# A decoder layer on one core: TensorE's instructions pinned to program order in the attention stage, and the column-tiled products gathered

## The chip, the cores and the metric

The kernel runs on 1 core of one Trainium2 chip. The metric is the device time of one execution in microseconds (us); the figure of the kernel before is the median of 3 runs.

## The reference, cut to what matters

One layer of a trunk with two kinds of heads, for a prompt of 2048 rows and for 8 sample rows with a cache of 2048 positions. All in fp32.

```python
u = x @ w_in              # 1024 -> 3584: q_a k_a v_a (attention), q_r k_r v_r g_r (retention)
# A: 8 heads x 64; each query attends in three branches (window, dilation) = (128,1) (512,4) (2048,16)
logits = q_a . k_a * 64**-0.5 + rel_bias[bucket(distance)];  p = softmax(logits);  o = p @ v_a
#    the branches are mixed by softmax of their log-sum-exp
# B: retention, 4 heads, dk = dv = 128, chunks of 128, decay gamma_h
scores = (q_r k_r^T) * decay;  o = scores @ v_r + (q_r @ state) * decay
state  = gamma**128 * state + k_dec^T @ v_r;   y = groupnorm(o) * silu(g_r)
x1  = LN1(alpha*x + concat(A, B) @ w_out)
out = LN2(alpha*x1 + relu(x1 @ w_up)**2 @ w_down)
```

The eight sample rows go through the same layer, with their keys and values from the cache and their own retention state.

## The kernel before, in words

Every fp32 operand of a large product is split into a high and a low part (`split`, line 348: the high part by ScalarE at line 351, the low part by VectorE at line 356), and each product is three matmuls (lines 343 to 345 in `gemm`, 441 to 443 in `gemm_flip`). The span falls into two parts. Up to about 1110 us **attention runs**: the input projection goes over the prompt in four blocks j of 512 rows, 28 weight tiles each (`gemm_phase`, line 388), with an output projection of 8 tiles after block 1 (block 0's rows) and three more after block 3. From then on the rest of the output projections, the layer norms and the feed-forward part run.

A weight tile is 24 matmuls of 512 rows (in block 0 two runs of 24 with 256 and 264 rows). Value tiles go the other way round (`gemm_flip`), two weight tiles for two halves. In each tile there is one **mid** point, halfway through it, and one **end** point behind the evacuation of its bank; at the last two tiles of a phase, which run interleaved, the two ends follow each other with no gemm between. Each of the four head pairs t has 7 tiles: q and k of attention (A), two of v (V), rotary q and k of retention (R), the gate (G). Blocks 1 and 2 take them in the order A V R G, blocks 0 and 3 in an order of their own, which ends in V, A, R, G of the last pair.

- `attn_advance` (line 699) is what a mid does: the products with v (`attn_pv`, line 664, matmuls of line 687) of the step before last, the transposes (`attn_tr`, line 656) of the last one, the products q k (`attn_qk`, lines 630 and 631) of the next. A pair has 4 such steps in blocks 0 and 1 and 6 in blocks 2 and 3, 80 in all. Between q k and the transposes lie VectorE's bias and minimum (line 644) and ScalarE's exp (line 645).
- `end` (line 1452) takes one job from each of four lists: loads of v, `fin0` to `fin4` (the mix of the branches), the retention stages `r0` to `r4` of `ret_stages` (line 795), and the sample rows' jobs (`sample_jobs`, line 863). The retention stages are appended at the end of the pair's last R or V tile, so that `r0` runs at the end after that, `r1` one end later, and so on: `r0` transposes the rotary keys (line 804), `r1` makes the decayed scores (line 811) and the state's update (lines 817 and 823), `r2` the output (lines 830 and 831) and its norm (lines 835 to 843), `r3` transposes that (line 850).
- `pair_begin` (line 467) runs what is left of the pair before, with nothing between the steps.
- `w_split` (line 162) splits a weight tile two tiles ahead; in block 0 it also makes the sample rows' v (`v_sample`, line 556, matmuls of line 562, summed by VectorE at lines 543 and 545).

**Two shapes of matmul.** Most use all 128 columns of the array. The products with v use 64 (one head of the pair each, side by side), and those of the sample rows 32 or 8 (lines 562, 981, 991, 1026, `tile_position`). In this document a run of such column-tiled products with no other matmul between is a *visit*.

**Banks.** PSUM pools have two banks each: `pg` for the gemm, `po` for the sums of the products with v, `ps` for q k and for the banks `rs`, `rd`, `ro` of `r1` and `r2`, `pt` for the transposes and the sample rows.

**Order.** The program is written in this order, but a scheduler then orders each engine's instructions, by priority (program order) among those that its own model of time holds ready. TensorE's order in the trace is thus not that of the program.

Of the kernel before, what the change touches and what calls it, by code (L numbers as in the profile page):

```python
# [60 lines left out]
class Trunk:  # L61
# [105 lines left out]
    def w_split(self, k):  # L167
        if k in self.wraw:
            nc = self.nc
            h = self.wp.tile([P, 1024], F32R, tag="wh", name=f"wh{k}", bufs=3)  # L170
            l = self.wp.tile([P, 1024], F32R, tag="wl", name=f"wl{k}", bufs=3)
            w = self.wraw.pop(k)
            if k in self.vsk:
                self.v_sample(*self.vsk[k], w)
            for c in range(0, 1024, 256 if k == 0 else 1024):
                c = slice(c, c + (256 if k == 0 else 1024))
                self.split(h[:, c], l[:, c], w[:, c], "s", "v")
            if self.at is None:
                self.busy(A=0.95, D=1.13)
            self.wrdy[k] = (h, l)  # L180
# [151 lines left out]

    def gemm(self, ps, w, x, c0, n, mid=None, ks=None):

        mm = self.nc.tensor.matmul
# [52 lines left out]
    def gemm_phase(self, nm, evac, mid, end, nxt=None, pre=None, before_next=None, flip=lambda m: 0):  # L388
# [3 lines left out]
        for m in range(nm - 1):  # L392
# [35 lines left out]
    def gemm_flip(self, m, evac, mid, end):  # L428

        mm = self.nc.tensor.matmul  # L430
        ws = [self.w_next() for _ in range(2)]
        ws = [tuple(x[:, k * 256:(k + 1) * 256] for x in w) for w in ws for k in range(4)]
        for half in range(2):
            ps = self.bank(self.pg, "vps")
            for b in range(2):
                if b:
                    mid(m + half)
# [10 lines left out]
    def attn_open(self):  # L448
# [13 lines left out]
        self.steps, self.sa, self.sb = [], None, None  # L462
# [76 lines left out]
    def ev_v(self, t, half, ps):  # L539
        nc, at = self.nc, self.at  # L540
        if half is None:
            v = at.tile([P, 512], F32, tag="p", name=self.nm("svn"), bufs=4)[:NB, :256]
            nc.vector.tensor_copy(v, ps[0:NB])
            for g in range(1, 4):
                nc.vector.tensor_tensor(out=v, in0=ps[32 * g:32 * g + NB], in1=v, op=OP.add)
            sl = slice(t * P, (t + 1) * P)
# [9 lines left out]
    def v_sample(self, t, half, w):  # L556

        if half == 0:
            self.vsp = self.bank(self.pt, "vss", 256)
        for k in range(4):  # L560
            g = 32 * k
            self.nc.tensor.matmul(self.vsp[g:g + NB], self.xs[:, 4 * half + k, :], w[:, 256 * k:256 * k + 256],
                                  start=(half == 0), stop=(half == 1), tile_position=(0, g))
        if half:
            self.ev_v(t, None, self.vsp)
# [28 lines left out]
    def attn_qk(self, s):  # L594
# [4 lines left out]
        for x in range(2):  # L599
# [4 lines left out]
            for ui, u in enumerate(s["units"]):  # L604
# [25 lines left out]
                nc.tensor.matmul(o, lh, rhs, start=True, stop=False)  # L630
                nc.tensor.matmul(o, ll, rhs, start=False, stop=True)
# [17 lines left out]
    def attn_tr(self, s):  # L649
# [3 lines left out]
        for x in range(2):  # L653
            b = self.bank(self.pt, "ptps", tot)
            for k in range(tot // P):
                nc.tensor.transpose(b[:, k * P:(k + 1) * P], s["P"][x][:, k * P:(k + 1) * P], self.ident)
# [7 lines left out]
    def attn_pv(self, s):  # L664
# [6 lines left out]
        for (col, w), u in zip(s["w"], s["units"]):  # L671
            nk = w // P
            for k in range(nk):
                for x in range(2):
# [12 lines left out]
                    nc.tensor.matmul(out, v, s["PT"][x][:, col + k * P:col + (k + 1) * P],  # L687
# [48 lines left out]
    def fin2(self, c):  # L736
        nc = self.nc
        b = self.bank(self.pt, "aps", P, 16)
        nc.tensor.transpose(b, c["a"].rearrange("p x w b -> p (x w b)"), self.ident)
# [55 lines left out]
    def ret_stages(self, h, j):  # L795
# [4 lines left out]
        def r0():  # L800
            c["kn"] = at.tile([P, 4, P], F32, tag="kn", name=self.nm("kn"))
            b = self.bank(self.pt, "rtp")
            for i in range(4):
                nc.tensor.transpose(b[:, i * P:(i + 1) * P], k[:, i * P:(i + 1) * P], self.ident)
            nc.scalar.activation(c["kn"].rearrange("p a c -> p (a c)"), b, AF.Copy, scale=GAMMA_C[h])

        def r1():
            b = self.bank(self.ps, "rs")
            for i in range(4):
                sl = slice(i * P, (i + 1) * P)  # L810
                nc.tensor.matmul(b[:, sl], k[:, sl], q[:, sl], start=True, stop=True)
            c["A"] = at.tile([P, 4, P], F32, tag="ra", name=self.nm("ra"))
            nc.vector.tensor_tensor(out=c["A"], in0=b.rearrange("p (b n) -> p b n", n=P),
                                    in1=self.mask[:, None, :].to_broadcast([P, 4, P]), op=OP.mult)
            b = self.bank(self.ps, "rd")
            for i in range(4):
                nc.tensor.matmul(b[:, i * P:(i + 1) * P], c["kn"][:, i], v[:, i, 1], start=True, stop=True)
# [3 lines left out]
            for i in range(4):  # L821
                dst = S[:, i + 1] if i < 3 else self.state[:, h]
                nc.vector.scalar_tensor_tensor(out=dst, in0=S[:, i], scalar=GAMMA_C[h], in1=b[:, i * P:(i + 1) * P],
                                               op0=OP.mult, op1=OP.add)

        def r2():
            b = self.bank(self.ps, "ro")
            for i in range(4):
                sl = slice(i * P, (i + 1) * P)
                nc.tensor.matmul(b[:, sl], c["A"][:, i], v[:, i, 1], start=True, stop=False)  # L830
                nc.tensor.matmul(b[:, sl], q[:, sl], c["S"][:, i], start=False, stop=True)
# [15 lines left out]
        def r3():  # L847
            b = self.bank(self.pt, "ryt")
            for i in range(4):
                nc.tensor.transpose(b[:, i * P:(i + 1) * P], c["y"][:, i], self.ident)  # L850
# [9 lines left out]
        return [(r0, 1, 0), (r1, 0, 2), (r2, 0, 1), (r3, 1, 0), (r4, 0, 0)]  # L860


    def sample_jobs(self):
# [16 lines left out]
        def natural(g, m):  # L880
            def f():
                b = self.bank(self.pt, "snp", 512, NB)
                for t in range(4):
                    nc.tensor.transpose(b[:, t * P:(t + 1) * P], smp[:, t, m, :], self.ident)
# [44 lines left out]
        def soft1():  # L929
            b = self.bank(self.pt, "slt", 384, 64)  # L930
            for br in range(3):
                nc.tensor.transpose(b[:, br * P:(br + 1) * P], c["L"][:, br, :], self.ident)
# [19 lines left out]
        def soft2():  # L952
            b = self.bank(self.pt, "spt", 192)
            for br in range(3):
                nc.tensor.transpose(b[:, br * 64:(br + 1) * 64], c["ls"][:, br * P:(br + 1) * P],
# [14 lines left out]

        def pv(b):
            def f():
                vs = [c.pop(("vg", b, br)) for br in range(3)] + [c["n2"]]
                pm = at.tile([P, 4, 32], F32, tag="spm", name=self.nm("spm"), bufs=2)
                nc.gpsimd.memset(pm, 0.0)
                nc.gpsimd.tensor_copy(pm[:, 0:3, 0:8], c["pT"][:, :, b * 8:(b + 1) * 8])
                nc.vector.tensor_scalar(pm[0:NB, 3, 0:8], c["pn8"], self.ident[:NB, b:b + 1], None, op0=OP.mult)
                ps = self.bank(self.pt, "spv")
                for g in range(4):
                    k = P if g < 3 else NB  # L980
                    nc.tensor.matmul(ps[32 * g:32 * g + 32, :], pm[:k, g, :], vs[g], start=True, stop=True,
                                     tile_position=(0, 32 * g))
# [4 lines left out]

            def g():
                ps = self.bank(self.pt, "spd", P)
                for t in range(4):  # L990
                    nc.tensor.matmul(ps[32 * t:32 * t + 32, :], self.sc[:, 10:11].to_broadcast([P, 32]),
                                     c["so"][:, t * P:(t + 1) * P], start=True, stop=True, tile_position=(0, 32 * t))
                row(ps, self.hrow[0][b:b + 1].rearrange("b (t d) -> (b t) d", t=4))
                if b + 1 < NB:
                    for br in range(3):
                        v = ring("svg")
                        gather(b + 1, br, 1, v)
                        c["vg", b + 1, br] = v
            return [f, g]
# [10 lines left out]
        def ret(h, bh):  # L1010
            def f():
                s, vb = c.pop(("st", h, bh))
                nc.gpsimd.tensor_scalar(s, s, GAMMA[h], None, op0=OP.mult)
# [7 lines left out]
            def g():  # L1021
                s = c["new"]
                ps = self.bank(self.pt, "sro", P)
                for k in range(4):
                    b = 4 * bh + k
                    nc.tensor.matmul(ps[32 * k:32 * k + 32, :], c["rot"][:, h, 0, b:b + 1].to_broadcast([P, 32]),
# [4 lines left out]
                n = 2 * h + bh + 1  # L1031
                if n < 8:
                    ret_load(n // 2, n % 2)
# [5 lines left out]
        def gate():  # L1039
            b = self.bank(self.pt, "snp", 512, NB)  # L1040
            for t in range(4):
                nc.tensor.transpose(b[:, t * P:(t + 1) * P], smp[:, t, 6, :], self.ident)
# [26 lines left out]
        def last():  # L1069
            b = self.bank(self.pt, "shs", KT * NB)  # L1070
            for k in range(KT):
                src = (c["hw"] if k < 4 else c["hr"])[:, k % 4 * P:(k % 4 + 1) * P]
                nc.tensor.transpose(b[:, k * NB:(k + 1) * NB], src, self.ident[:NB, :NB])
# [5 lines left out]
        js += [soft1, soft2]  # L1079
        for b in range(NB):  # L1080
            js += pv(b)
        js += [ret_first]
        for h in range(4):
            for bh in range(2):
                js += ret(h, bh)
        js += [gate, norm, last]
        self.hrow = [self.dram(f"hrow{g}", [NB, 512]) for g in range(2)]
        return [(f, 1, 0) for f in js]
# [164 lines left out]
    def run(self):  # L1253
# [13 lines left out]
        for j, o_ in enumerate(self.order):  # L1267
            wseq += [win[7 * t + w] for t, w in o_] + wout * {1: 1, 3: 3}.get(j, 0)
# [627 lines left out]
```

## Time and profile before

| | |
|---|---|
| median of 3 runs | 2621.09 us (2619.31 to 2622.74) |
| the profiled execution | 2621.11 us, its span 2619.3 us |
| mean granted TensorE clock | 0.994 |
| busy: TensorE / its weight loads / VectorE / ScalarE | 98% / 91% / 68% / 48% |
| attention runs | to about 1110 us |

A line of the profile's groups gives source line, engine, operation, output and inputs by the program's names, shapes, count, then busy time and mean ns of one, then the engine's idle time before it and what ended it. A line of the timeline gives start and length in us; the end of a matmul is modelled, so the distance between two starts is what counts. An fp32 matmul of the attention stage shows as two records. A line of the stages gives, for each engine, busy time and count, then the granted clock (PEclk).

### The profile page before, as it was taken

The page shows a single profiled execution, that of the slowest core. Times are in us where ns is not written, and L with a number is a line of the kernel's source. Part 1 is how long each engine was busy: PE and PEld are TensorE (multiplying, and loading weights), DVE is VectorE, ACT ScalarE, POOL GpSimd, SP SyncE. Part 2 cuts the span into 40 slices and gives each one's busy share as a digit, 9 for nine tenths or more (in the row PEclk, how much of TensorE's full clock was granted, in tenths as well). Part 3 has the DMA queues.
Part 4 walks back from the last instruction along what each step waited for, and adds up shares of the span by engine and source line. Part 5 has one row for each costly group of instructions (what it writes and reads, how often), then busy time and mean ns, then how long its engine had stood idle before and what let it go on. Part 6 is the DMA issues. An engine that isn't in the chain of part 4 may idle for free.

```text
span 2619.3 us, 44506 instructions
## 1 busy us (share of the span) xinstructions
PE 2571.3 (98%) x16852; PEld 2380.0 (91%) x16852; DVE 1778.6 (68%) x3751; ACT 1260.3 (48%) x2632; POOL 89.2 (3%) x119
## 2 busy tenths in 40 slices
PE   8999999999999999989999999999999999999998
PEld 7999778877788788788999999999999999999998
DVE  5677886655676766679888666578775547755567
ACT  4456445444443555445565433356654336544336
POOL 0000320000110000000000000100000010000000
PEclk9999999999999999999999999999999999999999
DMA  7345764664666344578557332854484295433322
GB/s 257 115 127 181 225 184 145 210 212 141 190 193 202 117 152 148 163 228 280 204 185 261 119 113 101 306 190 153 158 265 133 93 301 197 164 111 102 100 89 76
DMA packets 233099, 451.36 MB, mean 172 GB/s; under 512 B 33665, under 2 KB 122434, under 8 KB 232339
## 3 DMA queue, kind: packets, MB, share of 16 engines
q1 hardware_dynamic: 210532, 403.07, 47.5%
q0 software_dynamic: 12864, 32.20, 3.9%
q10 hardware_dynamic: 9488, 13.24, 1.5%
q8 instruction: 133, 2.18, 0.4%
q14 instruction: 82, 0.67, 0.1%
HBM read 346.30 MB, written 102.12 MB: 171 GB/s over the span
## 4 chain that ended last, share of the span: by engine, by line
PE 51%; DMA 2%; DVE 2%; ACT 1%; issue 0%; SPq 0%; DVEq 0%; ACTq 0%
PE dps L1662 9%; PE dps L1663 9%; PE dps L1664 9%; PE ups L1603 7%; PE ups L1604 7%; PE ups L1605 7%; DMA xr<-hd 1%; PE gps L343 1%; PE gps L344 1%; PE gps L345 1%; DMA fr<-in_w_up 0%; DVE zc L1216 0%; DMA zc<-x1d 0%; DVE zc L1188 0%; DVE wl L356 0%
## 5 line engine op out<-in xcount | busy, mean ns | idle before, releaser
L1662 PE MATMUL dps<-hid,fh 128*128 128x344 f32 (+2 forms) x1544 | 487.9, 318 | 3.0 <-ACT fh L351 2.6
L1663 PE MATMUL dps<-hid,fh 128*128 128x344 f32 (+2 forms) x1544 | 490.3, 318 | 0.0
L1664 PE MATMUL dps<-hid,fl 128*128 128x344 f32 (+2 forms) x1544 | 480.0, 318 | 0.0
L1603 PE MATMUL ups<-fx,fu 128*128 128x344 f32 (+1 forms) x1344 | 429.1, 320 | 1.1 <-DVE rl L1627 0.7
L1604 PE MATMUL ups<-fx,fu 128*128 128x344 f32 (+1 forms) x1344 | 429.8, 320 | 0.0
L1605 PE MATMUL ups<-fx,fu 128*128 128x344 f32 (+1 forms) x1344 | 421.7, 319 | 0.8 <-DVE fu L356 0.6
L343 PE MATMUL gps<-xh,wh 128*128 128x512 f32 (+2 forms) x1120 | 398.7, 360 | 19.7 <-ACT xh L351 12.6
L345 PE MATMUL gps<-xh,wl 128*128 128x512 f32 (+2 forms) x1120 | 396.9, 355 | 0.9 <-DVE wl L356 0.8
L344 PE MATMUL gps<-xl,wh 128*128 128x512 f32 (+2 forms) x1120 | 397.0, 356 | 0.5 <-DVE xl L356 0.5
L351 ACT ACTIVATE fu<-fr 128x512 fp32r<-128x512 f32 x320 | 192.8, 627 | 348.1 <-PE dps L1663 235.0
L1671 DVE TENSOR_TENSOR ya<-dps,ya 128x344 f32<-128x344 f32 (+2 forms) x344 | 170.9, 504 | 194.7 <-PE dps L1664 192.8
L1662 PEld LDWEIGHTS dps<-hid,fh 128*128 128x128 f32 x1544 | 290.2, 188 | 3.5 <-ACT fh L351 2.9
L1663 PEld LDWEIGHTS dps<-hid,fh 128*128 128x128 f32 x1544 | 290.9, 188 | 0.0
L1664 PEld LDWEIGHTS dps<-hid,fl 128*128 128x128 f32 x1544 | 288.2, 188 | 0.2 <-DVE fl L356 0.2
L343 PEld LDWEIGHTS gps<-xh,wh 128*128 128x128 f32 x1120 | 212.7, 191 | 56.8 <-ACT xh L351 14.6
L1603 PEld LDWEIGHTS ups<-fx,fu 128*128 128x128 f32 x1344 | 252.6, 188 | 1.7 <-DVE rl L1627 1.0
L1604 PEld LDWEIGHTS ups<-fx,fu 128*128 128x128 f32 x1344 | 252.6, 188 | 0.0
L1605 PEld LDWEIGHTS ups<-fx,fu 128*128 128x128 f32 x1344 | 251.3, 188 | 1.3 <-DVE fu L356 1.3
L344 PEld LDWEIGHTS gps<-xl,wh 128*128 128x128 f32 x1120 | 213.7, 191 | 34.3 <-issue 5.4
L356 DVE TENSOR_TENSOR fu<-fr,fu 128x512 fp32r<-128x512 f32 x320 | 214.4, 690 | 43.0 <-ACT fu L351 41.1
L345 PEld LDWEIGHTS gps<-xh,wl 128*128 128x128 f32 x1120 | 213.7, 191 | 31.6 <-DVE wl L356 2.4
L356 DVE TENSOR_TENSOR wl<-wr,wh 128x1024 fp32r<-128x1024 f32 (+1 forms) x147 | 177.4, 1209 | 57.9 <-ACT wh L351 57.1
(256 smaller groups left out, 4269.6 us busy)
## 6 DMA issues: line engine op xcount, KB each, us to landing
wr<-in_w_in SPq DMA_DIRECT2D x111, 512.0 KB
fr<-in_w_down SPq DMA_DIRECT2D x96, 512.0 KB
fr<-in_w_up SPq DMA_DIRECT2D x64, 512.0 KB
fr<-wsd SPq DMA_DIRECT2D x64, 512.0 KB
xr<-in_x SPq DMA_DIRECT2D x64, 256.0 KB
wr<-in_w_out SPq DMA_DIRECT2D x32, 512.0 KB
wsd<-fr SPq DMA_DIRECT2D x48, 256.0 KB
t<-modd SPq DMA_DIRECT2D x16, 512.0 KB
```

Of the source, the lines that this page charges most:

```text
L343: mm(ps, wh, xh[:, c0:c0 + n], start=(k == 0), stop=False)
L344: mm(ps, wh, xl[:, c0:c0 + n], start=False, stop=False)
L345: mm(ps, wl, xh[:, c0:c0 + n], start=False, stop=(k == last))
L351: nc.scalar.activation(h, raw, AF.Copy)
L356: (nc.vector if eng_l == "v" else nc.gpsimd).tensor_tensor(out=l, in0=raw, in1=f32(h), op=OP.subtract)
L1603: mm(ps, wh, xh[:, k, :n], start=start and k == 0, stop=False, skip_group_check=not start)
L1604: mm(ps, wh, xl[:, k, :n], start=False, stop=False, skip_group_check=not start)
L1605: mm(ps, wl, xh[:, k, :n], start=False, stop=k == 3, skip_group_check=not start)
L1662: mm(ps, wh, xh, start=(k == 0), stop=False)
L1663: mm(ps, wh, xl, start=False, stop=False)
L1664: mm(ps, wl, xh, start=False, stop=(k == 3))
L1671: nc.vector.tensor_tensor(out=y, in0=ps, in1=y, op=OP.add)
```

## The change

- `pin` puts each of TensorE's instructions, through `mm` and `tr`, behind the one traced before it on TensorE, as long as `pinned` is set: from the second tile of block 0 on until the attention stage's memory is closed. All matmuls and transposes of `gemm`, `gemm_flip`, attention, retention and sample rows go through them. The other engines' orders stay with the scheduler.
- `attn_advance` keeps the steps whose transposes are made in a list `sb` and makes their products with v when there are two, or when no step is coming.
- The sample rows' v products wait in `vsq` for the next mid and stand first there, each half with its own bank and sum. Their weight tile is split a little earlier, ahead of that mid.
- 24 of the sample rows' jobs (those with column-tiled matmuls: `f` and `g` of `pv`, 16, and `g` of `ret`, 8) are marked "part": `end` doesn't take them; `attn_advance` takes one behind the products with v or behind the sample rows' v, or at the second mid in a row without either.
- `r1` makes the state's update first and the scores after it. The weights of a sample row's product with v (`prep`) are made one job earlier, and its state and cache rows are loaded one job earlier.

```diff
@@ w_split
             if k in self.vsk:
-                self.v_sample(*self.vsk[k], w)
+                self.vsq.append((*self.vsk[k], w))
@@
+    def pin(self, ins):
+        return self.tc.keep_in_program_order(ins) if self.pinned else ins
+
+    def mm(self, *a, **k):
+        return self.pin(self.nc.tensor.matmul(*a, **k))
+
+    def tr(self, *a):
+        return self.pin(self.nc.tensor.transpose(*a))
...
@@ gemm_phase, in the loop over k
+                        if k == len(w) // 2 and self.wdue in self.vsk:
+                            self.w_split(self.wdue)
@@ v_sample
-        if half == 0:
-            self.vsp = self.bank(self.pt, "vss", 256)
+        vsp = self.bank(self.pt, "vss", 256)
         for k in range(4):
             g = 32 * k
-            self.nc.tensor.matmul(self.vsp[g:g + NB], self.xs[:, 4 * half + k, :], w[:, 256 * k:256 * k + 256],
-                                  start=(half == 0), stop=(half == 1), tile_position=(0, g))
-        if half:
-            self.ev_v(t, None, self.vsp)
+            self.mm(vsp[g:g + NB], self.xs[:, 4 * half + k, :], w[:, 256 * k:256 * k + 256], start=True, stop=True,
+                    tile_position=(0, g))
+        self.ev_v(t, "s%d" % half, vsp)
@@ attn_advance
-        if self.sb is not None:
-            self.attn_pv(self.sb)
-            self.sb = None
+        part = bool(self.vsq)
+        for v in self.vsq:
+            self.v_sample(*v)
+        self.vsq = []
+        if len(self.sb) == 2 or (self.sb and self.sa is None):
+            part = True
+            for s in self.sb:
+                self.attn_pv(s)
+            self.sb = []
+        if self.smpj and self.smpj[0][1] == "part":
+            self.late += 1
+            if part or self.late == 2:
+                self.smpj.pop(0)[0]()
+                self.late = 0
         if self.sa is not None:
             self.attn_tr(self.sa)
-            self.sb, self.sa = self.sa, None
+            self.sb.append(self.sa)
+            self.sa = None
         if self.steps:
             self.sa = self.steps.pop(0)
             self.attn_qk(self.sa)
@@ r1: the bank rs, its four matmuls and the mask (c["A"]) move behind the bank rd and the state
...
@@ pv(b): prep(b) leaves f; the gathers of row b + 1 and prep(b + 1) move from g to the end of f
...
@@ ret(h, bh): ret_load of the next moves from the end of g to the start of f
...
@@ sample_jobs
-        return [(f, 1, 0) for f in js]
+        return [(f, "part" if f in part else 1, 0) for f in js]
@@ end_in, block 0, second tile
                     self.load_tables(0)
+                    self.pinned = True
@@ ffn_open
-        self.at = None
+        self.at, self.pinned = None, False
@@ end
-            if q and q[0][1] <= t and q[0][2] <= s:
+            if q and q[0][1] != "part" and q[0][1] <= t and q[0][2] <= s:
```

More of the change, by code (lines that the diff above doesn't have):

```diff
@@ L540, in ev_v @@
         nc, at = self.nc, self.at
[L541 to L544, printed above, removed]
+        if half in ("s0", "s1"):
+            if half == "s0":
+                self.svn = at.tile([P, 512], F32, tag="p", name=self.nm("svn"), bufs=4)[:NB, :256]
+                nc.vector.tensor_copy(self.svn, ps[0:NB])
+            v = self.svn
+            for g in range(half == "s0", 4):
                 nc.vector.tensor_tensor(out=v, in0=ps[32 * g:32 * g + NB], in1=v, op=OP.add)
+            if half == "s0":
+                return
             sl = slice(t * P, (t + 1) * P)
@@ L803, in r0 @@
             for i in range(4):
-                nc.tensor.transpose(b[:, i * P:(i + 1) * P], k[:, i * P:(i + 1) * P], self.ident)
+                self.tr(b[:, i * P:(i + 1) * P], k[:, i * P:(i + 1) * P], self.ident)
             nc.scalar.activation(c["kn"].rearrange("p a c -> p (a c)"), b, AF.Copy, scale=GAMMA_C[h])
         def r1():
[L808 to L814, printed above, removed]
             b = self.bank(self.ps, "rd")
             for i in range(4):
-                nc.tensor.matmul(b[:, i * P:(i + 1) * P], c["kn"][:, i], v[:, i, 1], start=True, stop=True)
+                self.mm(b[:, i * P:(i + 1) * P], c["kn"][:, i], v[:, i, 1], start=True, stop=True)
             S = at.tile([P, 4, P], F32, tag="rst", name=self.nm("rst"))
@@ L824, in r1 @@
                                                op0=OP.mult, op1=OP.add)
+            b = self.bank(self.ps, "rs")
+            for i in range(4):
+                sl = slice(i * P, (i + 1) * P)
+                self.mm(b[:, sl], k[:, sl], q[:, sl], start=True, stop=True)
+            c["A"] = at.tile([P, 4, P], F32, tag="ra", name=self.nm("ra"))
+            nc.vector.tensor_tensor(out=c["A"], in0=b.rearrange("p (b n) -> p b n", n=P),
+                                    in1=self.mask[:, None, :].to_broadcast([P, 4, P]), op=OP.mult)
         def r2():
@@ L969, in row, with prep @@
             nc.sync.dma_start(dst, r.rearrange("(g i) d -> g i d", i=32)[:, 0, :])
+        def prep(b):
+            pm = c["pm"] = at.tile([P, 4, 32], F32, tag="spm", name=self.nm("spm"), bufs=2)
+            nc.gpsimd.memset(pm, 0.0)
+            nc.gpsimd.tensor_copy(pm[:, 0:3, 0:8], c["pT"][:, :, b * 8:(b + 1) * 8])
+            nc.vector.tensor_scalar(pm[0:NB, 3, 0:8], c["pn8"], self.ident[:NB, b:b + 1], None, op0=OP.mult)
         def pv(b):
@@ L973, in f @@
                 vs = [c.pop(("vg", b, br)) for br in range(3)] + [c["n2"]]
[L974 to L977, printed above, removed]
+                pm = c["pm"]
                 ps = self.bank(self.pt, "spv")
@@ L986, in f @@
                                         in1=self.sc[:, 2:10, None].to_broadcast([P, 8, 64]), op=OP.mult)
[L988 to L993, printed above, removed]
                 if b + 1 < NB:
@@ L998, in g @@
                         c["vg", b + 1, br] = v
+                    prep(b + 1)
+            def g():
+                ps = self.bank(self.pt, "spd", P)
+                for t in range(4):
+                    self.mm(ps[32 * t:32 * t + 32, :], self.sc[:, 10:11].to_broadcast([P, 32]),
+                            c["so"][:, t * P:(t + 1) * P], start=True, stop=True, tile_position=(0, 32 * t))
+                row(ps, self.hrow[0][b:b + 1].rearrange("b (t d) -> (b t) d", t=4))
             return [f, g]
@@ L1078, in sample_jobs @@
         js += [logit(b, br) for b in range(NB) for br in range(3)]
-        js += [soft1, soft2]
+        js += [soft1, soft2, lambda: prep(0)]
+        part = []
         for b in range(NB):
             js += pv(b)
+            part += js[-2:]
         js += [ret_first]
```

53 lines of the change are left out of this document (29 added, 24 removed).

## The prediction

> **What bounds the kernel now.** I read the page first, then the stages, then TensorE's timeline in the attention stage, and last who waits for whom.
>
> ```profile
> span 2619.3 us, 44506 instructions
> PE 2571.3 (98%) x16852; PEld 2380.0 (91%) x16852; DVE 1778.6 (68%) x3751; ACT 1260.3 (48%) x2632; POOL 89.2 (3%) x119
> ```
>
> TensorE (PE) is busy all the time; only less work on TensorE, or fewer of its waits, can move the end. The profiled execution took 2621.11 us, 1.8 us outside its span, and the median of the runs is 2621.09 us, so a sum against this trace needs no correction. By stages:
>
> ```profile
> 60.00:330.00 270.00, 263.44 (x2090) 239.05 (x2088) 198.16 (x545) 140.42 (x373) 23.33 (x19) 1.00 0.52 160
> 960.00:1110.00 150.00, 150.00 (x969) 122.12 (x969) 95.42 (x221) 75.74 (x157) 2.10 (x4) 1.00 0.50 161
> 1110.00:2619.00 1509.00, 1485.40 (x9431) 1468.32 (x9427) 1030.76 (x1935) 740.78 (x1458) 22.86 (x36) 0.99 0.51 171
> ```
>
> After 1110 us weight loads fill 97% of the time. The change touches nothing there, and I take that stage at no change. While attention runs, weight loads fill only 81 to 89% though matmuls overlap without a gap: there TensorE spends time that is not work. The timeline shows where. Three visits, the first with 8 records (four products), the second with 16, the third with 16 in two pieces:
>
> ```profile
> 104.82 0.28 PE L344 MATMUL gps<-xl,wh 128*128 128x256 f32 x1
> 104.93 0.28 PE L345 MATMUL gps<-xh,wl 128*128 128x256 f32 x1
> 105.14 0.66 PE L687 MATMUL o<-ptile,v 128*64 128x128 f32 x8
> 105.73 0.44 PE L656 MATMUL ptps<-ident,p 128*128 128x128 f32 x2
> ...
> 291.21 0.40 PE L344 MATMUL gps<-xl,wh 128*128 128x512 f32 x1
> 291.45 0.39 PE L345 MATMUL gps<-xh,wl 128*128 128x512 f32 x1
> 291.77 1.09 PE L687 MATMUL o<-ptile,vv 128*64 128x128 f32 x16
> 292.79 0.65 PE L656 MATMUL ptps<-ident,p 128*128 128x128 f32 x4
> ...
> 300.03 0.40 PE L345 MATMUL gps<-xh,wl 128*128 128x512 f32 x1
> 300.36 0.43 PE L687 MATMUL o<-ptile,v 128*64 128x128 f32 x2
> 300.72 0.66 PE L656 MATMUL ptps<-ident,p 128*128 128x128 f32 x4
> 301.14 0.48 PE L343 MATMUL gps<-xh,wh 128*128 128x512 f32 x1
> 301.46 0.39 PE L344 MATMUL gps<-xl,wh 128*128 128x512 f32 x1
> 301.78 1.09 PE L687 MATMUL o<-ptile,v 128*64 128x128 f32 x14
> 302.79 0.66 PE L656 MATMUL ptps<-ident,p 128*128 128x128 f32 x4
> ```
>
> Read distances between starts. Two full matmuls of 512 rows stand 0.24 us apart (291.21 to 291.45); into a visit it is 0.32 or 0.33 (291.45 to 291.77, 300.03 to 300.36), and with 256 rows 0.21 in place of 0.11: **0.09 us to enter**. Eight records hold TensorE 0.59 us, sixteen 1.02: eight more cost 0.43, so 0.59 has **0.16 us that belongs to the visit**, at its first product and its way out. The matmul behind a visit is late too (301.14 to 301.46: 0.32 in place of 0.23): **0.05 to 0.09**. Together about 0.33 us. Where the scheduler lets the first product go alone, because it holds the other head's operand not ready, it is worse: 0.36 and 1.01 us in place of 1.02, so 0.35 more inside, a second entrance and a second way out of 0.09 and 0.06: **0.5 us for a split**.
>
> Counted in this timeline, there are 155 visits, from
>
> ```profile
> 19.71 1.04 PE L562 MATMUL vss<-wr,xs 128*8 128x256 f32 x8
> ...
> 1109.62 1.09 PE L687 MATMUL o<-ptile,v 128*64 128x128 f32 x14
> ```
>
> and 42 of them are such lone firsts. So visits cost 113 x 0.33 + 42 x 0.5 = 58 us.
>
> The Trainium skill, TensorEngine Tiling (Array Packing), section Key Properties, has a rule for this: changing the tiling mode, not just the tile, drains TensorE. By it, going from 64 to 32 columns inside a visit is a change of mode too.
>
> **Part by part. Fewer visits.** In program order a step's products can't be split by other work. 80 steps, two to a visit, make 40 visits. (Blocks 0 and 1 have two per pair, blocks 2 and 3 three: 16 + 24.) The sample rows' v has 8 halves, a mid each: 8 visits of their own, as these mids mostly hold no products with v. The 24 parts are taken at every visit and at the second mid without one; in blocks 2 and 3 three mids of seven have visits and one of the four others becomes late, so a quarter of the parts, and one or two in the output projection before, stand alone: 8. Makes 56 visits at 0.33, 18.5 us, and 16 parts inside a visit, for which I take the 0.16 of a first product and way out: 2.6 us. 58 - 21 = **-37 us** (-33 if half the parts stand alone).
>
> By the skill's rule an appended part pays a full drain and refill, 0.33 rather than 0.16; the sum would be 2.7 us higher. No run here isolates that.
>
> **What order hid.** Now TensorE waits where the scheduler used to put gemm matmuls, and all of them queue behind the waiting one. I went through each place where the program asks for a result sooner than other engines give it.
>
> *r2 and the next q k.* `r2` holds a bank of `ps` until its norm is made, and half a tile later the next pair's first step wants both banks. Before, the second head's q k slid behind gemm:
>
> ```profile
> 394.51 0.38 PE L831 MATMUL ro<-rst,rot 128*128 128x128 f32 x2
> 397.95 0.28 PE L630 MATMUL sps<-kst,qnh 128*128 128x256 f32 x1
> 401.96 0.29 PE L630 MATMUL sps<-kst,qnh 128*128 128x256 f32 x1
> ...
> 395.62 0.89 DVE L835 BATCH_NORM_STATS2 bs<-ro 128x6 f32<-128x128 f32 x4
> 398.24 1.37 DVE L843 TENSOR_SCALAR ry<-ro,mv,rsd 128x128 f32<-128x128 f32 x4 [0.60 <-ACT rsd L840]
> ```
>
> The norm ends at 399.61, 5.1 us after `r2`'s last product. In program order the second head asks after 12 gemm matmuls (12 x 0.233 = 2.8) and the first head's four (4 x 0.12): 3.3 us. The wait is 1.8 us as here, where VectorE had key work between; from L835 on the chain took 4.0 us, and without that work (two pieces, about 1.4 us, partly under ScalarE's turn) it is near 3.5 us, a wait of about 0.3. It happens at 14 of the 16 `r2` (not after the last pair of blocks 1 and 2, where no step follows). I take 0.9: **+12 us** (4 to 25).
>
> *r0 at the end of a phase.* The last rotary tile of a block ends together with the last tile, and `r0` stands right behind, ahead of the next phase's gemm. Before, it ran 10 us later. It needs five VectorE operations on the tile:
>
> ```profile
> 490.45 0.68 DVE L775 TENSOR_TENSOR rot<-gps,cs 128x512 f32<-128x512 f32 x1
> 491.14 0.69 DVE L776 TENSOR_TENSOR rt<-gps,cs 64x512 f32<-64x512 f32 x1
> 491.85 0.68 DVE L777 TENSOR_TENSOR rt<-gps,cs 64x512 f32<-64x512 f32 x1
> 494.31 0.69 DVE L778 TENSOR_TENSOR rot<-rot,rt 128x512 f32<-128x512 f32 x1
> 496.72 0.69 DVE L779 TENSOR_TENSOR rot<-rot,dec 128x512 f32<-128x512 f32 x1
> ...
> 500.55 0.60 PE L804 MATMUL rtp<-ident,rot 128*128 128x128 f32 x4
> ```
>
> 3.4 us back to back, 7.0 as they lay here, between splits of the next rows. Three phases end so (blocks 1, 2, 3); block 0 has its second part of 256 rows only, about 2.1. 3 x 3.4 + 2.1 = 12.3 us, and a wait of that length halves the clock afterwards:
>
> ```profile
> 327.00:330.20 3.20, 0.84 (x8) 0.64 (x6) 3.12 (x5) 1.57 (x2) 0.67 (x1) 0.98 0.47 133
> 330.20:337.00 6.80, 5.93 (x28) 5.94 (x29) 6.74 (x10) 2.66 (x5) 3.81 (x3) 0.51 0.44 128
> ```
>
> Idle for 2.4 of 3.2 us, TensorE got 0.51 of its clock for 6.8 us and lost 3.3 us. I take half of that at two of the phases: **+16 us** in all (7 to 30).
>
> The Trainium skill, TensorE: Matmul & The Clock Gate, section "Why this matters for your kernels", speaks against the change here: no idle gaps over about 3 us between bursts, or the clock goes back to half. The trace agrees (the row of 0.51). By that rule all three gaps of 3.4 us pay and the one of 2.1 us doesn't; 1.7 us more than my sum.
>
> *Smaller ones.* At the end of block 0 two mids stand three matmuls apart, and the second's transposes need the first's exp; in block 3 `pair_begin` twice runs a step with nothing behind it; and the sample rows' sums keep a bank of `pt` that the transposes want.
>
> ```profile
> L644 DVE CUSTOM_DVE_ANT_1 p<-sps,t 128x256 f32<-128x256 f32 x120 | 45.7, 418 | 20.7 <-PE sps L631 20.3
> L645 ACT ACTIVATE p<-p,st 128x256 f32<-128x256 f32 x152 | 75.9, 500 | 104.7 <-DVE st L644 104.6
> L545 DVE TENSOR_TENSOR svn<-vss,svn 8x256 f32<-8x256 f32 x9 | 3.8, 420 | 0.3
> ```
>
> Four L644 and a last exp are 2.2 us: one wait of about 2 us in block 0, two of about 1 in block 3. Four operations on the sum are 1.7 us, less the first head's transposes, 0.4: 1.3 us, three times with transposes in the same mid. **+8 us** (0 to 20; 0 if they fall under one another).
>
> **What goes.** `r1` starts the state first, so the waits for it shrink:
>
> ```profile
> PE ro L831 <- DVE rst L823: 4.6, 3, 3.2
> ```
>
> The longest, 3.2 us, is the one before the half clock above. 4.6 + 3.3, and 2 us of lesser waits in the attention stage that lie out of program order: **-10 us** (-4 to -15). The earlier loads and `prep` fall on SyncE, GpSimd and VectorE off the path: nothing; without that cover a sample row's part would wait for its gather, about 2 us each.
>
> **Sum:** -37 + 12 + 16 + 8 - 10 = -11 us; 2621.1 - 11 = **2610 us**.
>
> **The rivals.** *It goes smoothly* (2588 us): VectorE serves the norm and the rotary tile at once, since fewer results are wanted out of turn; of the waits remain 12.3 at the phases and 2 or 3 elsewhere: -37 + 14 - 10 = -33. For it: TensorE's waits in the stage are few now. Against: VectorE is busy 73% of 60 to 330 us, and the five rotary operations now lie spread over 7 us.
>
> *The norm's bank decides the other way* (2642 us): if VectorE comes to L835 late, behind key work and splits, each of the 14 waits at the second head's q k is 2.5 us, and every third drops the clock to half for one stretch of 3.4 us: 35 + 5 x 1.7 = 43.5 in place of my 12, and -37 + 43.5 + 16 + 8 - 10 = +20.5. It decides from 1.6 us a wait on, where 14 waits eat the 23 us that the other terms leave. For it: that one norm at 5.1 us, a wait of 1.8. Against: program order gives the norm priority over what follows it.
>
> *The change doesn't do what it says* (2621 us): if the pairs of steps don't meet, or parts and sample rows mostly stand alone, some 90 visits at 0.33 remain, and -28 with 12 + 16 + 8 - 10 is about nil.
>
> **How the numbers follow.** 0.2%, 5.2 us, is about what a measurement of this kernel can tell from no change. The forecast with its neighbourhood (2596 to 2622) has 0.40, three quarters of it below 2615.9; the smooth case 0.25; the norm's bank 0.23; no merging 0.12, three quarters of it the same. Faster 0.30 + 0.25 + 0.03 = 0.58, same 0.10 + 0.09 = 0.19, slower 0.23. The range takes in the smooth case and half of the slow one: 2584 to 2637.
>
> **What would show it.** In the changed kernel: 50 to 70 visits, none with a lone first product of a step, most with 20 to 32 records; weight loads over 85% of 60 to 330 us. Waits of the second head's L630 for L843's line, 14 of them, 12 us in sum; `r0` waiting 3 to 4 us for the rotary tile at three phases, with half clock behind. The prediction is wrong if the waits named are under 10 us or over 50 us in sum, if more than 90 visits remain, or if the stage after attention changes by over 5 us.

## The result, and the profile after

| | before | after |
|---|---|---|
| median | 2620.35 us (2619.31 to 2622.74, 4 runs) | 2715.28 us (2708.0 to 2716.42, 4 runs) |
| mean granted clock of the profiled execution | 0.994 | 0.973 |
| attention's last product with v | 1110 us | 1189 us |

The ratio is 1.0355 (95% interval 1.0335 to 1.0375): 3.6% slower, 95 us, where 2610 us was forecast. The page of the changed kernel:

```profile
span 2714.0 us, 44492 instructions
PE 2577.4 (95%) x16852; PEld 2405.1 (89%) x16852; DVE 1781.3 (66%) x3767; ACT 1264.5 (47%) x2632; POOL 85.6 (3%) x119
PEclk9999979999998899999999999999999999999999
```

The same 16852 matmul records, but TensorE's busy share went from 98% to 95%, and the granted clock dips in several slices. The stages, with the columns as before:

```profile
60.00:330.00 270.00, 244.32 (x1945) 228.37 (x1944) 176.78 (x512) 127.48 (x346) 8.50 (x8) 0.94 0.44 133
330.00:600.00 270.00, 235.79 (x1448) 199.92 (x1447) 167.02 (x383) 106.96 (x227) 30.41 (x31) 0.94 0.55 167
...
1230.00:2714.00 1484.00, 1464.17 (x9328) 1450.93 (x9326) 1014.45 (x1905) 731.51 (x1439) 22.87 (x36) 1.00 0.50 169
```

In 60 to 330 us TensorE was busy 263.4 of 270 us at clock 1.00 before; now 244.3 at 0.94. Behind attention weight loads fill 98% and the clock is 1.00, as good as before (97% and 0.99 in the last row of the stages). The loss is all in the attention stage: it is waits, and the clock that falls behind them. Who waits for whom, on TensorE, in the attention stage of the changed kernel (total us, times, longest; L342 is `tr`, L339 `mm`, so the tile names tell the step):

```profile
PE rtp L342 <- DVE rot L811: 27.1, 5, 10.2
PE ptps L342 <- ACT ptile L678: 12.2, 13, 4.2
PE ptps L342 <- ACT p L664: 7.9, 8, 2.8
PE ptps L342 <- DVE hr L884: 7.9, 5, 3.8
PE rtp L342 <- DVE es L759: 7.1, 1, 7.1
PE sps L339 <- issue: 6.7, 2, 3.4
PE sps L339 <- DVE ry L875: 6.3, 4, 2.6
...
PE ro L339 <- DVE rst L848: 3.2, 1, 3.2
```

The largest line of this view before was 4.6 us. For the whole stage I took the distance from each matmul record's start to the next, and subtracted the distance that equal records have in an undisturbed run at full clock (0.233 us for 512 columns, 0.0545 for a product with v). More than 0.45 us left over counts as a wait; less, inside a half-clock stretch, as lost clock; what lies at and between column-tiled records as the cost of visits. The work itself is 1019 us before and 1015 after:

| attention stage, us | visits | cost of visits | waits (count) | lost at half clock | other |
|---|---|---|---|---|---|
| before, 12 to 1130 | 155 | 48.6 | 23.9 (20) | 6.2 | 20.3 |
| after, 12 to 1220 | 58 | 11.7 | 119.5 (64) | 45.6 | 16.2 |

Visits gave 37 us, waits took 96, the clock 39, the rest gave 4: +94 us. (The 4 us between the two sums of work I put down to where the stretches are cut.) The waits by the tile that the waiting instruction writes: `rtp` (`r0`) 38.2 us in 7, `ptps` (transposes of P) 36.9 in 31, `sps` (q k) 24.4 in 13, all others 20.

Two of them closely. At the end of block 1 the last gemm matmul is followed by `r0`, in TensorE's timeline:

```profile
540.41 0.40 PE L339 MATMUL gps<-xh,wl 128*128 128x512 f32 x1
547.95 1.08 PE L342 MATMUL rtp<-ident,rot 128*128 128x128 f32 x4 [7.15 <-DVE es L759]
...
549.26 0.63 PE L339 MATMUL gps<-xl,wh 128*128 128x512 f32 x1
549.69 0.63 PE L339 MATMUL gps<-xh,wl 128*128 128x512 f32 x1
```

TensorE stands for over 7 us, though the gemm of the next phase is there (kernel 3 below moves this `r0` and has no wait at the same end). Behind it two matmuls of 512 columns stand 0.43 us apart (549.26 to 549.69) in place of 0.233: half clock. VectorE in the same time:

```profile
540.15 0.69 DVE L807 TENSOR_TENSOR rot<-gps,cs 128x512 f32<-128x512 f32 x1 [0.70 <-PE gps L339]
...
541.56 0.68 DVE L809 TENSOR_TENSOR rt<-gps,cs 64x512 f32<-64x512 f32 x1
542.28 0.69 DVE L368 TENSOR_TENSOR xl<-xr,xh 128x512 fp32r<-128x512 f32 x1
...
542.96 2.36 DVE L368 TENSOR_TENSOR wl<-wr,wh 128x1024 fp32r<-128x1024 f32 x2
545.23 0.69 DVE L810 TENSOR_TENSOR rot<-rot,rt 128x512 f32<-128x512 f32 x1
...
546.52 0.68 DVE L825 TENSOR_TENSOR g<-gps,ge 128x512 f32<-128x512 f32 x1
547.12 0.68 DVE L811 TENSOR_TENSOR rot<-rot,dec 128x512 f32<-128x512 f32 x1
547.72 0.17 DVE L759 TENSOR_TENSOR es<-d,st 128x16 f32<-128x16 f32 x1
```

The five rotary operations are 3.4 us of work, but take from 540.15 to 547.80, 7.7 us, since splits of the next rows and weights lie between them. (`es` L759, named as the releaser, starts at 547.72 and only ends last; the tile `rot` is what `r0` reads.) The longest wait, 10.2 us in block 1's first pair, has the same form, and there VectorE had itself stood behind a transfer that its queue came to first, with all five rotary operations behind that (340.26 to 348.27):

```profile
339.05 0.69 DVE L784 TENSOR_TENSOR o1s<-o1s,ab 128x512 f32<-128x512 f32 x1 [4.98 <-DMA ab<-ad]
```

Of the small waits 13 are of this kind (`ptps` <- `ptile` above):

```profile
536.73 0.60 PE L342 MATMUL ptps<-ident,p 128*128 128x128 f32 x4
538.06 0.66 PE L342 MATMUL ptps<-ident,p 128*128 128x128 f32 x4 [0.73 <-ACT ptile L678]
```

The second head's transposes start when ScalarE has copied the first head's out of `pt`, and in program order no gemm matmul may fill the 0.73 us.

### The profile page after: what moved, and what is told of

Its sections match the earlier page's. It is cut to its first block, busy times and chain, and to the rows that moved or that the text cites. A ratio compares the mean times of both kernels' runs of the same rounds, so it can differ in the third digit from the quotient of the medians.

```text
span 2714.0 us, 44492 instructions
## 1 busy us (share of the span) xinstructions
PE 2577.4 (95%) x16852; PEld 2405.1 (89%) x16852; DVE 1781.3 (66%) x3767; ACT 1264.5 (47%) x2632; POOL 85.6 (3%) x119
## 3 DMA queue, kind: packets, MB, share of 16 engines
q1 hardware_dynamic: 210532, 403.07, 45.6%
## 4 chain that ended last, share of the span: by engine, by line
PE 76%; DMA 11%; DVE 8%; ACT 2%; issue 2%; SPq 1%; POOL 0%; DVEq 0%; ACTq 0%; POOLq 0%
PE gps L339 16%; PE dps L1703 8%; PE dps L1705 8%; PE dps L1704 8%; PE ups L1644 7%; PE ups L1645 7%; PE ups L1646 7%; PE vps L339 5%; PE sps L339 2%; PE o L339 2%; PE ptps L342 2%; DMA ab<-ad 2%; DMA skg<-in_cache 1%; DVE wl L368 1%; DMA xr<-hd 1%
## 5 line engine op out<-in xcount | busy, mean ns | idle before, releaser
L339 PE MATMUL gps<-xh,wh 128*128 128x512 f32 (+2 forms) x1120 | 412.3, 370 | 14.7 <-ACT xh L363 10.1
L339 PE MATMUL gps<-xl,wh 128*128 128x512 f32 (+2 forms) x1120 | 404.3, 361 | 1.4 <-DVE xl L368 1.4
L339 PE MATMUL gps<-xh,wl 128*128 128x512 f32 (+2 forms) x1120 | 401.1, 359 | 2.7 <-DVE wl L368 2.7
L339 PEld LDWEIGHTS gps<-xh,wh 128*128 128x128 f32 x1120 | 220.5, 198 | 50.0 <-ACT xh L363 12.4
L339 PEld LDWEIGHTS gps<-xh,wl 128*128 128x128 f32 x1120 | 220.0, 197 | 34.6 <-DVE wl L368 3.1
L339 PEld LDWEIGHTS gps<-xl,wh 128*128 128x128 f32 x1120 | 221.3, 198 | 32.0 <-DVE xl L368 3.1
L363 ACT ACTIVATE wh<-wr 128x1024 fp32r<-128x1024 f32 (+1 forms) x147 | 151.3, 1036 | 167.2 <-PE gps L339 123.6
```

What stands on the lines that cost most here:

```text
L339: return self.pin(self.nc.tensor.matmul(*a, **k))
L363: nc.scalar.activation(h, raw, AF.Copy)
```

## The experiments

**Theory 1**: waits in program order are the whole loss (with the clock that they cost), and the visits' gain is real. **Rivals**: the gathering itself (later products, held banks) makes the waits; or merged visits are worth little. Times are medians; each ratio is against the kernel before, run beside it on the same chip (2619.84 us for 1 to 4, 2617.33 for 5 to 8, 2619.3 for 9 and 10). The last four columns are the split of the attention stage as above.

| kernel | us | ratio (95%) | visits | their cost | waits | half clock |
|---|---|---|---|---|---|---|
| 1 gathered, order free | 2619.41 | 1.0001 (0.9986 to 1.0016) | 123 | 37.2 | 31.9 | 11.0 |
| 2 kept in order, not gathered | 2725.37 | 1.0405 (1.0381 to 1.0429) | 112 | 22.6 | 123.6 | 37.3 |
| 3 `r0` one end later | 2680.69 | 1.0235 (1.0209 to 1.026) | 58 | 11.4 | 100.0 | 32.6 |
| 4 gemm free | 2650.45 | 1.0125 (1.0106 to 1.0144) | 140 | 41.3 | 49.1 | 14.8 |
| 5 order free, head by head | 2615.89 | 0.9995 (0.9986 to 1.0004) | 69 | 33.9 | 27.4 | 15.0 |
| 6 before, head by head | 2628.61 | 1.005 (1.0037 to 1.0062) | 114 | 59.7 | 24.6 | 8.3 |
| 7 transposes free | 2687.72 | 1.0262 (1.0243 to 1.0281) | 62 | 13.3 | 100.5 | 30.8 |
| 8 q k free | 2658.49 | 1.016 (1.0145 to 1.0176) | 59 | 12.1 | 81.1 | 22.9 |
| 9 order free, later head first | 2599.19 | 0.9923 (0.9909 to 0.9937) | 69 | 14.5 | 32.3 | 15.8 |
| 10 before, later head first | 2605.45 | 0.9942 (0.9928 to 0.9955) | 117 | 30.0 | 27.5 | 4.8 |

**1 and 2: each half of the change alone.** The first is the changed kernel with the order left to the scheduler:

```diff
-                    self.pinned = True
+                    self.pinned = False
```

> The changed kernel with nothing pinned: gathered products, sample rows' jobs and the r1 order stay, TensorE's order is the scheduler's again. Theory 1 (the pinned order makes the waits): waits over 0.45 us in the attention stage fall from 119.5 us to about the 24 us of before, half clock from 126 us to under 30; 65 to 100 visits, because the scheduler may still part a visit; 2590 to 2608 us. Theory 2 (the gathering makes the waits, because two steps hold their operands and banks longer): waits stay over 60 us and the time over 2640 us.

The second is the kernel before with `pin`, `mm` and `tr` over the same stretch and nothing gathered.

> The kernel before with TensorE pinned to program order in the same stretch, and nothing else of the change. Theory 1: waits of 95 to 130 us and 100 us or more at half clock as in the changed kernel, visits about 110 (80 of v, 32 of the sample rows less those that meet), so 15 us more than the changed kernel: 2720 to 2745 us. Theory 2: waits under 60 us, under 2670 us.

Keeping the order alone costs 105 us (2725.37 against 2619.84); gathering alone costs and gives nothing in sum (2619.41): its visits are 11 us cheaper, its waits 8 us and its lost clock 5 us higher than before. So the gathering doesn't make the loss, and the first rival falls. TensorE's waits in the second kernel:

```profile
PE rtp L340 <- DVE rot L788: 25.7, 5, 7.7
PE ro L337 <- DVE rst L832: 9.5, 3, 5.7
...
PE rtp L340 <- DVE den L739: 8.6, 1, 8.6
PE ptps L340 <- ACT ptile L668: 7.3, 9, 2.1
```

It is the same `r0` wait, 25.7 us in 5 here and 27.1 in 5 in the changed kernel. Among the kernels kept in order, gathering gives 10 us (+105 to +95, each against its own runs of the kernel before), and visits fall from 112 to 58 and 22.6 to 11.7 us. Their waits are alike in sum (123.6 and 119.5) but not in place: at the transposes of P they are 17.4 us in 15 in kernel 2 and 36.9 in 31 with the gathering, where fewer mids have products with v ahead of the transposes. That this is the reason was not tested. In the first kernel the scheduler parts what was gathered: 123 visits, 31 of them a lone product.

**3: the largest wait moved.** An empty stage ahead of the last pair's `r0` in blocks 0, 1 and 3 lets it run one end later, behind a tile of gemm:

```diff
+                        if t == NRET - 1 and j != 2:
+                            self.rets.append((lambda: None, 0, 0))
```

> The changed kernel with r0 of the last pair one end later in blocks 0, 1 and 3 (behind the first tile of the next phase). Theory 1 with the waits adding up: the three waits of 6.8, 7.3 and 6.5 us at those phase ends go, and with each one stretch of half clock (1.7 to 3.4 us): 2715 - 20 - 8 = 2687 us. Rival: what waits is VectorE's backlog, which the next instruction in order then meets (the evacuations or q k): the waits move and the time stays over 2705 us.

34 us of the added time went. By the split 19.5 us are waits and 13 us lost clock: a wait costs over half as much again in clock.

**4: gemm alone free.** Everything else is kept in order; the gemm's matmuls may come earlier.

```diff
-        mm = self.mm
+        mm = self.nc.tensor.matmul
```

> The changed kernel with only the matmuls and transposes of attention, retention and sample rows pinned, each behind the one traced before it; the gemm's matmuls are free to come earlier. Theory 1: gemm fills the waits again, which fall under 50 us, half clock under 50 us, visits 55 to 75: 2595 to 2640 us. Theory 2: as the changed kernel, over 2690 us.

A miss: waits fell to 49 us, but the gemm then went into the visits as well (140, 41 lone products), and the time stayed above the range. Which parts cost what was left to 7 and 8.

**7 and 8: one kind of step free.** All is kept in order among itself, but the transposes of P (7) or q k (8) go where the scheduler puts them (for that `pin` ties each kept instruction to the kept one before it; this part of the edit isn't shown):

```diff
-                self.tr(b[:, k * P:(k + 1) * P], s["P"][x][:, k * P:(k + 1) * P], self.ident)
+                nc.tensor.transpose(b[:, k * P:(k + 1) * P], s["P"][x][:, k * P:(k + 1) * P], self.ident)
```

```diff
-                self.mm(o, lh, rhs, start=True, stop=False)
-                self.mm(o, ll, rhs, start=False, stop=True)
+                nc.tensor.matmul(o, lh, rhs, start=True, stop=False)
+                nc.tensor.matmul(o, ll, rhs, start=False, stop=True)
```

> The changed kernel with everything kept in order but the attention's transposes of P, which the scheduler may put where it likes (62 visits in place of 58). Theory 1 (each kind of step adds waits of its own, and clock with them): the waits of the transposes, 36.9 us in 31, go, and their share of the half clock (39 us of clock for 96 us of added waits, so about 15 us): 2715 - 52 = 2663 us; with some of the waits handed on to the next step kept in order 2655 to 2690 us. Rival (the wait only moves to what stands behind, since ScalarE and VectorE deliver no sooner): 2700 to 2720 us.

> The changed kernel with everything kept in order but q k, which the scheduler may put where it likes (59 visits). Theory 1: the waits of q k, 24.4 us in 13, go, and their share of the half clock, about 10 us: 2715 - 34 = 2681 us (2672 to 2700). Rival (the wait for the bank moves on to the transposes behind): 2705 to 2720 us.

Both came out below their rivals' ranges, by 12 and 46 us. The transposes were worth 25 us, at the small end of what was expected; q k 54 us, more than expected and 14 us below the range stated. The waits of the transposes with them free:

```profile
PE ptps L680 <- ACT ptile L683: 15.8, 4, 7.3
```

13 small waits became 4 long ones. As I read it, the scheduler's model of time holds the bank free earlier than ScalarE's copy delivers it, and puts the transposes too early. And with q k free:

```profile
PE sps L654 <- DVE st L668: 7.2, 8, 3.7
PE ptps L347 <- ACT ptile L683: 5.2, 4, 3.3
...
PE ptps L347 <- ACT p L669: 2.9, 4, 1.8
```

q k opens the step's chain (q k, minimum, exp, transposes). All waits at `ptps` fell from 36.9 us to 11.0, beside those of q k from 24.4 to 9.4. So part of what I count under the transposes goes with q k. Where it goes early the transposes find their P ready more often (`ptps` <- `p`, 7.9 us to 2.9); why the waits for ScalarE's copy fell as well (12.2 to 5.2) is not shown. Against their own runs of the kernel before, the changed kernel stands at +95 us and 3, 7 and 8 at +61, +70 and +41: they took 34, 25 and 54 us, 113 together.

**5 and 6: whole visits without an order.** A visit is parted because its first product is ready before its last. If the product whose operand comes last (the second head's, copied by VectorE) goes first, all others are ready when it is. Kernel 5 is kernel 1 with the later step first and in it the second head's products, then the first's (its longer edit isn't shown); kernel 6 is the kernel before with the same order of heads:

```diff
-        for (col, w), u in zip(s["w"], s["units"]):
-            nk = w // P
-            for k in range(nk):
-                for x in range(2):
+        for x in (1, 0):
+            for (col, w), u in zip(s["w"], s["units"]):
+                nk = w // P
+                for k in range(nk):
```

> The changed kernel with the scheduler's order (nothing kept), and in each visit the product first whose operand comes last: the later step's second head, then the others. When that operand is there all are, so a visit should stay whole without any pinning. Theory 1 (the gathered visits are worth what the prediction said, the order's waits ate it, and in the first experiment the scheduler parted the visits again): about 70 visits in place of 123, none with a lone first; entering, leaving and inside 37 us there and 12 us at 58 visits in the changed kernel, so about 16 us here; waits as in the first experiment (32 us and 11 us of half clock). 2619.4 - 21 = 2598 us (2588 to 2608). Rival (merging is worth little by itself; what was saved in the changed kernel's visits came from the order): 2619 us, within 5.

> The kernel before with one edit: the products with v of a step go head by head, the second head's (copied by VectorE, later) first, the scheduler free as before. Nothing is gathered and nothing kept in order. Theory 1: the lone firsts go (47 before, 5 or so left), 114 visits in place of 155; 41 splits at 0.5 us, so -20 us: 2600 us (2594 to 2610). Rival (a split costs nothing where TensorE has other work): 2620 us, within 4. A second rival: the visit starts later, as it waits for the later head's copy, the bank of the transposes is freed as before, nothing else moves: no loss from it, under 3 us.

Both missed: 2615.89 us, where the rival had it, and 2628.61, above every range, though the visits came out whole (69 and 114). The split shows why: inside the visits 16.5 and 30.1 us over the work, before 8.4. A visit of 32 records in kernel 5:

```profile
291.27 1.25 PE L339 MATMUL o<-ptile,vv 128*64 128x128 f32 x13 [0.59 <-DVE ptile L680]
...
292.97 0.87 PE L339 MATMUL o<-ptile,vv 128*64 128x128 f32 x8
293.77 1.09 PE L342 MATMUL ptps<-ident,p 128*128 128x128 f32 x8
```

From 291.27 to 293.77, 2.50 us at full clock. My edit had changed a second thing: products of one head follow each other, where they had alternated between the two halves of the columns.

**9 and 10: the same, alternating.** Only the pair's order is turned; in kernel 9 the later step also goes first:

```diff
-                for x in range(2):
+                for x in (1, 0):
```

> The fifth experiment's kernel (gathered, order free, 69 visits) with the two heads' products alternating again, each pair with the second head (the later operand) first. In the fifth one the products went head by head, and its visits came out whole but slow inside: 16.5 us over the work, where the changed kernel's alternating ones had 2.6 us less than the work. Theory 1 (products that alternate between the two halves of columns overlap, those in a row on one half don't, and this took back what the whole visits gave): entering, leaving and inside 34 us there, about 15 here, so 2615.9 - 19 = 2597 us (2588 to 2606), 0.8% under the kernel before. Rival (whole visits are worth nothing when the order is free, because TensorE then waits for VectorE and ScalarE anyway): 2612 to 2620 us.

> The kernel before with one edit: in each pair of products with v the second head (the later operand) goes first, alternating as before; nothing gathered, nothing kept. 117 visits in place of 155, 7 lone firsts in place of 47. Theory 1: a split costs 0.5 us as the prediction had it, 40 fewer are -20 us; the sixth experiment, which went head by head, lost 38 us inside its visits beside its neighbour in this call's design: 2600 us (2593 to 2610). Rival (a split costs nothing; the sixth experiment's loss of 11 us was the later start): 2617 to 2628 us.

(The last text's "38 us inside" is a slip: kernel 6 lost 30.1 us inside its visits, 22 more than the kernel before.) The same visit in kernel 9:

```profile
294.79 1.09 PE L339 MATMUL o<-ptile,vv 128*64 128x128 f32 x16 [0.68 <-DVE ptile L680]
295.71 0.39 PE L339 MATMUL o<-ptile,v1prev 128*64 128x128 f32 x4
295.93 0.82 PE L339 MATMUL o<-ptile,vv 128*64 128x128 f32 x12
296.69 1.09 PE L342 MATMUL ptps<-ident,p 128*128 128x128 f32 x8
```

32 records from 294.79 to 296.69, 1.90 us. Both came out as theory 1 had it: 2599.19 us, 20 us under the kernel before, and 2605.45, 14 us under it. Kernel 9 is the fastest, ahead of the kernel before and of the changed one; its page:

```profile
span 2602.1 us, 44494 instructions
PE 2542.1 (98%) x16852; PEld 2379.8 (91%) x16852; DVE 1782.9 (69%) x3767; ACT 1259.7 (48%) x2632; POOL 89.8 (3%) x119
PEclk8999999999999999989999999999999999999999
```

TensorE is again busy 98%, with 29 us less of it than before. Its two longest waits are

```profile
PE ptps L342 <- DVE ptile L680: 6.1, 2, 4.9
PE ro L339 <- DVE ra L864: 4.6, 1, 4.6
```

## Why the prediction was wrong, point by point

- **Fewer visits, -37 us: right in sum.** 58 visits for 56 forecast, 48.6 us of cost to 11.7, where I had 58 to 21. Its parts were not right, so that the sum came out is partly luck: the splits were the larger part. 112 visits kept in order cost 22.6 us (kernel 2), 0.20 each, where I had 0.33. So no more parted visits is worth 26 us, and half as many only 11. Kernels 10 and 9 show the same without an order: 18.6 us by whole visits, 15.5 more by gathering. The waits and lost clock of kernel 9 are 16 us higher, which takes all of the latter; the 6 us between the two times lie in what the split leaves over. (The -33 that the prediction gives for half the parts alone doesn't follow from its own prices: eight more visits at 0.33 in place of 0.16 make -36. Nothing else rests on it.)
- **"What order hid": the step that failed.** I put 36 us on it, waits and clock, and it measured 119.5 us of waits with 45.6 of lost clock. I looked for places where the program asks too soon and named the three kinds of step that do wait; their sizes were wrong, and part of the causes.
  - *`r0`*: 12.3 us forecast, 38.2 measured. I took "3.4 us back to back", though the row quoted there said 7.0 as they lay. It was 7.7 us at block 1's end. The order of TensorE doesn't rearrange VectorE's queue: the splits still lie between. The 3.4 us lost to that queue is the term that I mis-read. And I looked at phase ends only; the longest wait, 10.2 us, stood at the first pair of block 1.
  - *q k*: 12 us in 14 waits forecast, 24.4 in 13 measured. The norm's bank, which I had as their cause, shows only 6.3 us in 4 (`ry` L875); the rest waits for other things.
  - *Smaller ones*: 8 us forecast, 36.9 at the transposes alone. I priced a few cases and left out two kinds at nothing: ScalarE's copy of the first head (12.2 us in 13 by the view of waits, mostly some 0.7 us, once 4.2) and the bank that `r3` holds until `hr` is made (7.9 in 5); the exp, which I had at three mids and some 4 us, took 7.9 in 8. No wait of the transposes stood in that view of before, since gemm went there. Kernel 8 adds that some of it goes with q k.
  - *Half clock*: 3.3 us added and 3.3 taken away in the forecast, 39 us more measured. I gave it to two long waits; TensorE fell to it 23 times, about half of them after waits of 3 us or less.
- **"What goes", -10 us: mostly failed.** The wait of 3.2 us for `rst` is still there (`ro` <- `rst` L848: 3.2, 1), with half clock behind it.
- **After attention: right.** The time over the work of its records, counted as in the split, is 39.5 us for 37.9 before.
- **The rivals.** The change did what it says (58 visits). The norm's bank was the wrong place for the loss. The smooth case (2588 us) had the right worth of visits; kernel 9 comes within 11 us of it, and only because nothing is kept in order. No rival had a price for many small waits, and none reached 2715 us.
- **The sign of being wrong** that I had named came: waits over 50 us in sum. Net of those that go they stood at 26 us in the forecast, against 96 added in the measurement, and the gap with its clock is the whole miss: 70 us of waits and 39 us of clock, less the 4 of the rest, 105 us, as between 2610 and 2715.

What stays open: how the added waits share out between q k and the transposes, since freeing one moves the other; and which of kernel 9's remaining 32 us of waits would go with a later `r2` or an earlier copy. Neither was tried.

## What to carry to other kernels

Where a scheduler fills one engine's waits, their price is hidden: before an order is fixed, every hand-over between engines is priced at the time that it takes in the trace, with all that lies in the other engine's queue, and not at the sum of its operations; short waits at each step count as much as the few long ones (here 53 waits under 3 us made 62 us, the eleven longer ones 58). If work should stay together, it can be enough to put first the piece whose operand comes last; here this gave 14 us alone and 20 with the gathering, where fixing the order lost 95. An order of loops may hold something up that isn't its purpose (here the alternation of the two halves), so an edit that changes two things is read from the trace before its theory is given up.

## What the runs showed of the hardware that was not expected

**Short waits halve the clock.** A wait of 1.67 us in the changed kernel, in TensorE's timeline and in the stages (clock in the third column from the right):

```profile
73.00 0.28 PE L339 MATMUL sps<-kst,qnl 128*128 128x256 f32 x1
74.95 0.55 PE L339 MATMUL sps<-kst,qnh 128*128 128x256 f32 x1 [1.67 <-DVE ry L875]
```

```profile
73.00:75.00 2.00, 0.34 (x4) 0.16 (x2) 1.97 (x6) 0.00 (x0) 0.00 (x0) 0.99 0.65 158
75.00:78.40 3.40, 3.40 (x16) 3.40 (x17) 3.25 (x14) 1.97 (x8) 0.00 (x0) 0.50 0.17 67
78.40:81.00 2.60, 2.60 (x23) 2.60 (x23) 0.83 (x2) 0.96 (x1) 0.00 (x0) 1.00 0.02 6
```

After it TensorE ran at 0.50 for 3.4 us. All stretches at half clock in the changed kernel are 3.4 us long or a multiple of that (3.4, 6.8, 10.2), 126 us in 23 stretches for 119.5 us of waits. Of the waits near 1.5 us some were followed by it and some not, and the trace shows a pattern: all changes of the clock lie on one grid with 3.41 us from point to point. From 30 us on to the end of attention the clock fell from full to half at 21 of these points, and at each TensorE had been idle for 1.57 us or more of the 3.41 us before, in one wait or several; at the points where it stayed full it had been idle for 1.42 us or less, but for one with 1.78. In the traces of the other kernels the two groups overlap between 1.0 and 1.9 us, so there is no sharp bound; but the idle time between two such points tells more than the length of one wait. No run was made to test this. The Trainium skill, TensorE: Matmul & The Clock Gate, section "Why this matters for your kernels", asks for no idle gaps over about 3 us. Here gaps of under 2 us were enough, so for this kernel that figure is too generous.

**Products that alternate between the halves of the columns overlap.** 32 records took 1.90 us alternating and 2.50 us head by head (kernels 9 and 5). In the visit of kernel 9 above the records start in pairs, 6 ns apart, with about 0.10 us to the next pair; in that of kernel 5 only three such pairs stand, and most distances are 0.05 to 0.11 us. The 16.5 us inside the visits of kernel 5 went to -2.4 (less than the work as I count it) in kernel 9, and the time fell by 17 us (19 against their own runs of the kernel before). The Trainium skill, TensorEngine Tiling (Array Packing), section Key Properties, says that different tiles can load weights and multiply in parallel. The two kernels agree with it.
